# Seven products instead of eight in a third pair of each gate and up unit, with the sums on the weights made by GpSimd

## The chip, the cores and the metric

The kernel runs on one core of a Trainium2 chip. The metric is the device time of one execution in microseconds (us). Five engines work on a core: PE (TensorE, the matrix multiplier), ACT (ScalarE), DVE (VectorE), POOL (GpSimd), and SP (SyncE), which here only issues transfers.

## The reference

One decoder layer on 256 tokens of width 2048 with 16 learned tokens ahead of them: a SwiGLU block, a mixer (differential attention beside a gated short convolution), a second SwiGLU block, a last norm. The change is in the first half of the second SwiGLU block, where gate and up are made:

```python
D_MODEL = 2048; SEQ = 256; D_FF = 5632
def swiglu_ffn(h, w_gu, w_down):
    gate, up = jnp.split(h @ w_gu, 2, axis=-1)
    return (jax.nn.silu(gate) * up) @ w_down
...
h = rms_norm(s, norm_ffn2[layer])
s = s + 0.5 * swiglu_ffn(h, ffn2_w_gu[layer], ffn2_w_down[layer])
```

All inputs are float32.

## The kernel before

Every float32 operand of a matmul is split into a high part that TensorE takes at full speed (type fp32r) and the low remainder; a product is three matmuls: high times high, low times high, high times low. Activations are split when they are made. Weights are split as they arrive: a tile `st` comes from memory by a transfer that SP issues, ACT writes the high part `wh` (a cast, line 369) and DVE the remainder `wl` (a subtraction, line 370). This is the helper `parts`. There are three buffers each for `wh` and `wl` (`W_BUFS`) and four for `st` (`ST_BUFS`).

The second block's inner width of 5632 is cut into 11 groups of 512. Group 0 is made by `linear_tok`, which on the way also writes the normalised activations `hn` (`renorm`, `Mixed.pair`). Groups 1 to 10 are made by `gate_up_mix`; one call is called a unit here. A unit makes gate and up, 512 columns each, for 256 tokens (two halves of 128), over 2048 rows of weights. `linear_mix` takes these rows as eight pairs of 128-row chunks. For one pair the work is a product of a 2 x 2 matrix of blocks (token half by chunk, 128 x 128 each) with a 2 x 2 matrix of weight blocks (chunk by gate or up, 128 x 512 each). The string `KINDS` says for each of the eight pairs how this is done:

- D (direct): eight block products, in two tiles of four (tile c holds chunk c's rows for gate and for up). A tile is 12 matmuls.
- S: Strassen's way in Winograd's form, seven block products. The four sums on the activations are made once, in `Mixed.pair`, and kept as `sp`. The four sums on the weights are made anew in every unit, in a tile `tt` that takes one of the four `st` buffers (lines 507 to 510; the third needs the first, the fourth needs the third). Its products come in four tiles: one of 3 matmuls and three of 6. The last two tiles are cast from `tt`.

The results of all pairs add up in eight PSUM banks, named 1 to 7 and x. `left` counts the products that a bank is still to get; at the last one `done` evicts it (lines 522 to 543, on ACT and DVE), most of them in pair 7. The sigmoid and two products for the whole unit (`gated`, lines 546 to 548) follow in the next unit's first pair, and the result is transposed on PE (`back`, lines 561 to 566) in that next unit's last pair.

`step` and `AHEAD` put the casts of two further tiles ahead of a tile's matmuls in program order; a framework then makes a fixed order for each engine and the semaphores. After groups 0 to 3, 4 to 7 and 8 to 10 stands the product with `w_down` for that third (`linear_tok`, named pd). Behind the last units GpSimd's queue holds two loads of the last norm's gains (`gfin`, line 928).

Of the kernel before, what the change touches and what calls it, by code (L numbers as in the profile page):

```python
# [36 lines left out]
WARM = 6  # L37
HOLD = 3
LATER_AT = (4, 6)
KINDS = "DDDSDDDS"  # L40
AHEAD = 2


# [1 line left out]
def decoder_layer(ctx: ExitStack, tc: tile.TileContext, t, out):  # L45
    nc = tc.nc
# [7 lines left out]
    def bank(name):  # L54
        return psum.tile([P, 512], F32, tag="acc", name=name)
# [179 lines left out]
    def step(use):  # L235

        ahead.append(use)
        drain(AHEAD)
# [62 lines left out]
    def flush():  # L301
        while pending:
            pending.pop(0)()
# [61 lines left out]
    def parts(src, n=2):  # L365

        wh = wpool.tile([P, 2, GW], F32R, tag="wh", name="wh")[:, :n, :]
        wl = wpool.tile([P, 2, GW], F32R, tag="wl", name="wl")[:, :n, :]
        nc.scalar.copy(out=wh, in_=src)  # L369
        nc.vector.tensor_sub(wl, src, wh.bitcast(F32))  # L370
        return wh, wl
# [49 lines left out]
    class Mixed:  # L421
# [6 lines left out]
        def pair(self, p, f):  # L428
# [4 lines left out]
            nc.vector.tensor_sub(tl[:, :, 1, :], f, tl[:, :, 0, :].bitcast(F32))  # L433
            if KINDS[p] == "S":
                a11, a12, a21, a22 = (f[:, c, i * P : (i + 1) * P] for i in range(2) for c in range(2))
# [13 lines left out]
    def linear_mix(a, w, cols, name, done):  # L449

        nd, ns = KINDS.count("D"), KINDS.count("S")
        left = {k: 2 * nd * (k in "234x") + ns * (k != "x") for k in "1234567x"}
        ps = {}

        def product(k, left_op, wh, wl):
            first = k not in ps
            if first:
                ps[k] = bank(name + k)
            left[k] -= 1
            hi, lo = left_op
            nc.tensor.matmul(ps[k], hi, wh, start=first, stop=False)  # L467
            nc.tensor.matmul(ps[k], lo, wh, start=False, stop=False)  # L468
            nc.tensor.matmul(ps[k], hi, wl, start=False, stop=left[k] == 0)  # L469
            if left[k] == 0:  # L470
                done(k, ps[k])

        def use(p, n, products):

            for k, left_op, wh, wl in products:
                product(k, left_op, wh, wl)
            if p == len(KINDS) - 1 and n in (1, 2) and later:
                later.pop(0)()
            if n == (1 if KINDS[p] == "D" else 3):
                if p == 0:  # L480
                    flush()
                if side:
                    side.pop(0)()

        for p, kind in enumerate(KINDS):
            st = wpool.tile([P, 2, 2, GW], F32, tag="st", bufs=ST_BUFS, name="st")
            rows = w[2 * p * P : (2 * p + 2) * P, :].rearrange("(c p) f -> p c f", p=P)
            for q in range(2):
                nc.sync.dma_start(out=st[:, :, q, :], in_=rows[:, :, cols[q] : cols[q] + GW])
            (a11, a21), (a12, a22) = ([a.block(2 * p + c, i) for i in range(2)] for c in range(2))  # L490
            if kind == "D":
                tiles = [
                    (st[:, c], (("2", a1, 0), ("3", a1, 1), ("4", a2, 0), ("x", a2, 1)))
                    for c, (a1, a2) in enumerate(((a11, a21), (a12, a22)))
                ]
            else:
                s1, s2, s3, s4 = a.sums[p]
                tt = wpool.tile([P, 4, GW], F32, tag="st", bufs=ST_BUFS, name="tt")
                tiles = [
                    (st[:, 1, 1:2, :], (("3", s4, 0),)),  # L500
                    (st[:, :, 0, :], (("1", a11, 0), ("2", a12, 1))),
                    (tt[:, 2:4, :], (("6", s2, 0), ("4", a22, 1))),
                    (tt[:, 0:2, :], (("5", s1, 0), ("7", s3, 1))),
                ]
            for n, (src, products) in enumerate(tiles):
                if kind == "S" and n == 2:
                    nc.vector.tensor_add(tt[:, 0, :], st[:, 0, 0, :], st[:, 0, 1, :])
                    nc.vector.tensor_add(tt[:, 2, :], tt[:, 0, :], st[:, 1, 1, :])
                    nc.vector.tensor_add(tt[:, 3, :], tt[:, 2, :], st[:, 1, 0, :])
                    nc.vector.tensor_add(tt[:, 1, :], st[:, 0, 1, :], st[:, 1, 1, :])  # L510
                wh, wl = parts(src, src.shape[1])
                products = [(k, left_op, wh[:, j, :], wl[:, j, :]) for k, left_op, j in products]
                step(lambda p=p, n=n, products=products: use(p, n, products))

    def gate_up_mix(a, w_gu, g, m, gi):
# [3 lines left out]
        def done(k, ps):  # L519
# [21 lines left out]
            elif k == "7":  # L541
# [10 lines left out]
                pending.append(gated)  # L552

        linear_mix(a, w_gu, (g * GW, F + g * GW), "pg", done)

    def back(act, g, mt, k):
# [421 lines left out]
```

## Time and profile before

| | |
|---|---|
| time, median of 3 runs (lowest to highest) | 2226.62 us (2225.67 to 2226.89) |
| profiled execution, its own time | 2225.46 us |
| span of the profiled execution (first to last instruction) | 2223.7 us |
| mean granted TensorE clock | 0.998 |
| busy: PE, DVE, ACT, POOL | 2205.9, 1376.3, 998.2, 6.4 us |
| the ten units with the down products between them | 1535 to 2150 us of the span |

Busy shares are of the whole span; the stages differ. "Idle before" is time that an engine stood still ahead of an instruction, and behind the arrow stands what ended it. In the windows, each engine's busy time is followed by its number of instructions. A matmul's duration is longer than the time until the next one can start, since they are pipelined; the spacing of starts is what counts. L370 is line 370 of the kernel.

### The profile page before, as it was taken

The page shows a single profiled execution, that of the slowest core. Times are in us where ns is not written, and L with a number is a line of the kernel's source. Part 1 is how long each engine was busy: PE and PEld are TensorE (multiplying, and loading weights), DVE is VectorE, ACT ScalarE, POOL GpSimd, SP SyncE. Part 2 cuts the span into 40 slices and gives each one's busy share as a digit, 9 for nine tenths or more (in the row PEclk, how much of TensorE's full clock was granted, in tenths as well). Part 3 has the DMA queues.
Part 4 walks back from the last instruction along what each step waited for, and adds up shares of the span by engine and source line. Part 5 has one row for each costly group of instructions (what it writes and reads, how often), then busy time and mean ns, then how long its engine had stood idle before and what let it go on. Part 6 is the DMA issues. An engine that isn't in the chain of part 4 may idle for free.

```text
span 2223.7 us, 33100 instructions
## 1 busy us (share of the span) xinstructions
PE 2205.9 (99%) x13608; PEld 1989.5 (89%) x13608; DVE 1376.3 (62%) x1792; ACT 998.2 (45%) x1244; POOL 6.4 (0%) x17
## 2 busy tenths in 40 slices
PE   9999999999999999999999999999999999999998
PEld 8999999999999999898988888888888888888886
DVE  7555554455555565667765554668776578846875
ACT  6444343334434443444444444455454445534544
POOL 0000000000000000000000000000000000000000
PEclk9999999999999999999999999999999999999999
DMA  7555455555555455444555555555566555665563
GB/s 233 176 180 176 171 172 178 181 171 171 176 180 175 171 171 186 156 142 144 170 189 189 190 189 189 177 184 172 188 200 200 187 190 189 208 211 182 178 225 113
DMA packets 192023, 401.95 MB, mean 181 GB/s; under 512 B 8676, under 2 KB 8736, under 8 KB 191872
## 3 DMA queue, kind: packets, MB, share of 16 engines
q1 hardware_dynamic: 191232, 398.49, 53.0%
q8 instruction: 106, 1.74, 0.3%
q0 software_dynamic: 544, 1.21, 0.2%
q14 instruction: 45, 0.37, 0.0%
q10 hardware_dynamic: 96, 0.14, 0.0%
HBM read 397.71 MB, written 2.10 MB: 180 GB/s over the span
## 4 chain that ended last, share of the span: by engine, by line
PE 97%; DVE 1%; ACT 1%; DMA 0%; issue 0%; ACTq 0%; DVEq 0%
PE pg L467 5%; PE pg L469 5%; PE pg L468 5%; PE pg L282 4%; PE pg L280 4%; PE pd L282 4%; PE pu L282 4%; PE pu L280 4%; PE pg L281 4%; PE pd L280 4%; PE pd L281 4%; PE pu L281 4%; PE pd L320 4%; PE pd L318 4%; PE pd L319 4%; PE o L278 3%
## 5 line engine op out<-in xcount | busy, mean ns | idle before, releaser
L271 DVE TENSOR_TENSOR wl<-st,wh 128x1024 fp32r<-128x1024 f32 x392 | 478.5, 1223 | 442.4 <-ACT wh L270 442.1
L270 ACT CAST wh<-st 128x1024 fp32r<-128x1024 f32 x392 | 411.4, 1050 | 613.9 <-PE pd L281 146.9
L370 DVE TENSOR_TENSOR wl<-st,wh 128x1024 fp32r<-128x1024 f32 (+1 forms) x360 | 426.9, 1192 | 280.0 <-ACT wh L369 279.1
L369 ACT CAST wh<-st 128x1024 fp32r<-128x1024 f32 (+1 forms) x360 | 368.3, 1030 | 472.3 <-PE pgx L468 154.9
L280 PE MATMUL pg<-h,wh 128*128 128x272 f32 x704 | 203.3, 290 | 2.0 <-ACT wh L270 2.0
L280 PE MATMUL pu<-h,wh 128*128 128x272 f32 x704 | 203.3, 289 | 0.0
L282 PE MATMUL pu<-h,wl 128*128 128x272 f32 x704 | 203.0, 288 | 0.0
L282 PE MATMUL pd<-m,wl 128*128 128x272 f32 x704 | 203.0, 288 | 0.0
L280 PE MATMUL pd<-m,wh 128*128 128x272 f32 x704 | 202.9, 288 | 0.0
L281 PE MATMUL pd<-m,wh 128*128 128x272 f32 x704 | 202.4, 288 | 0.0
L281 PE MATMUL pu<-h,wh 128*128 128x272 f32 x704 | 202.4, 288 | 0.0
L281 PE MATMUL pg<-h,wh 128*128 128x272 f32 x704 | 202.4, 288 | 0.0
L282 PE MATMUL pg<-h,wl 128*128 128x272 f32 x704 | 201.1, 290 | 0.0
L467 PE MATMUL pg<-wh,hn 128*128 128x512 f32 x420 | 163.6, 390 | 0.0
L468 PE MATMUL pg<-wh,hn 128*128 128x512 f32 x420 | 163.5, 389 | 0.0
L469 PE MATMUL pg<-wl,hn 128*128 128x512 f32 x420 | 160.3, 391 | 0.0
L318 PE MATMUL pd<-wh,m 128*128 128x512 f32 x352 | 137.6, 391 | 0.0
L319 PE MATMUL pd<-wh,m 128*128 128x512 f32 x352 | 137.0, 389 | 0.0
L320 PE MATMUL pd<-wl,m 128*128 128x512 f32 x352 | 135.9, 390 | 0.0
L280 PEld LDWEIGHTS pg<-h,wh 128*128 128x128 f32 x704 | 132.9, 189 | 2.3 <-ACT wh L270 2.3
L281 PEld LDWEIGHTS pg<-h,wh 128*128 128x128 f32 x704 | 133.3, 189 | 0.0
L281 PEld LDWEIGHTS pu<-h,wh 128*128 128x128 f32 x704 | 132.7, 189 | 0.0
(279 smaller groups left out, 4536.4 us busy)
## 6 DMA issues: line engine op xcount, KB each, us to landing
st<-in_ffn_w_gu_dram SPq DMA_DIRECT2D x184, 512.0 KB, 4.3
st<-in_ffn_w_down_dram SPq DMA_DIRECT2D x88, 1024.0 KB, 5.1
st<-in_ffn_w_gu_dram SPq DMA_DIRECT2D x84, 1024.0 KB, 4.8
st<-in_w_in_dram SPq DMA_DIRECT2D x48, 1024.0 KB, 5.1
st<-in_w_gate_dram SPq DMA_DIRECT2D x64, 512.0 KB, 4.3
st<-in_w_branch_dram SPq DMA_DIRECT2D x32, 512.0 KB, 4.5
st<-in_w_out_dram SPq DMA_DIRECT2D x16, 1024.0 KB, 5.0
xin<-in_x_dram SPq DMA_DIRECT2D x8, 256.0 KB, 7.3
```

The costliest lines, as they stand in the source:

```text
L270: nc.scalar.copy(out=wh[:, :m, :], in_=sw)
L271: nc.vector.tensor_sub(wl[:, :m, :], sw, wh[:, :m, :].bitcast(F32))
L280: nc.tensor.matmul(a, wh[:, i, f], act.part(c, 0, t0, t1), start=first, stop=False)
L281: nc.tensor.matmul(a, wh[:, i, f], act.part(c, 1, t0, t1), start=False, stop=False)
L282: nc.tensor.matmul(a, wl[:, i, f], act.part(c, 0, t0, t1), start=False, stop=last)
L318: nc.tensor.matmul(ps, hi, wh[:, q, :], start=first, stop=False)
L319: nc.tensor.matmul(ps, lo, wh[:, q, :], start=False, stop=False)
L369: nc.scalar.copy(out=wh, in_=src)
L370: nc.vector.tensor_sub(wl, src, wh.bitcast(F32))
L467: nc.tensor.matmul(ps[k], hi, wh, start=first, stop=False)
L468: nc.tensor.matmul(ps[k], lo, wh, start=False, stop=False)
L469: nc.tensor.matmul(ps[k], hi, wl, start=False, stop=left[k] == 0)
```

## The change

Pairs 2, 5 and 7 of each unit are S instead of pairs 3 and 7, so there are five D pairs and three S pairs. `Mixed.pair` follows `KINDS` and makes the activation sums for pairs 2, 5 and 7. The four sums on the weights are issued to GpSimd instead of VectorE, with the same operands and in the same place in the program.

```diff
-KINDS = "DDDSDDDS"
+KINDS = "DDSDDSDS"
...
                 if kind == "S" and n == 2:
-                    nc.vector.tensor_add(tt[:, 0, :], st[:, 0, 0, :], st[:, 0, 1, :])
-                    nc.vector.tensor_add(tt[:, 2, :], tt[:, 0, :], st[:, 1, 1, :])
-                    nc.vector.tensor_add(tt[:, 3, :], tt[:, 2, :], st[:, 1, 0, :])
-                    nc.vector.tensor_add(tt[:, 1, :], st[:, 0, 1, :], st[:, 1, 1, :])
+                    nc.gpsimd.tensor_add(tt[:, 0, :], st[:, 0, 0, :], st[:, 0, 1, :])
+                    nc.gpsimd.tensor_add(tt[:, 2, :], tt[:, 0, :], st[:, 1, 1, :])
+                    nc.gpsimd.tensor_add(tt[:, 3, :], tt[:, 2, :], st[:, 1, 0, :])
+                    nc.gpsimd.tensor_add(tt[:, 1, :], st[:, 0, 1, :], st[:, 1, 1, :])
```

## The prediction, made before the result was known

> **What bounds the kernel now.** I read the profile page first (busy times, chain), then the stage that the change touches (windows by unit, waits, DVE in order of time), then rows for single prices.
>
> ```profile
> span 2223.7 us, 33100 instructions
> PE 2205.9 (99%) x13608; PEld 1989.5 (89%) x13608; DVE 1376.3 (62%) x1792; ACT 998.2 (45%) x1244; POOL 6.4 (0%) x17
> ...
> PE 97%; DVE 1%; ACT 1%; DMA 0%; issue 0%; ACTq 0%; DVEq 0%
> ```
>
> The chain that ended last runs on PE for 97% of the span, and GpSimd (POOL) does almost nothing. So a matmul less is worth its spacing, unless DVE or ACT becomes late. DVE's 62% is a mean over stages; in the stage of the change it is otherwise. These windows are one gate and up unit each, from one unit's first transposes to the next one's:
>
> ```profile
> core 0: us, PE busy (x) PEld busy (x) DVE busy (x) ACT busy (x) POOL busy (x), PEclk, DMA share, GB/s
> 1574.96:1618.91 43.95, 43.53 (x197) 35.47 (x195) 35.38 (x41) 22.23 (x26) 0.00 (x0) 1.00 0.56 191
> 1618.91:1662.94 44.03, 43.61 (x197) 35.47 (x195) 35.43 (x41) 22.28 (x26) 0.00 (x0) 1.00 0.57 190
> ...
> 1603.11 0.39 PE L467 MATMUL pg<-wh,hn 128*128 128x512 f32 x1
> 1615.80 0.39 PE L469 MATMUL pg<-wl,hn 128*128 128x512 f32 x1
> ...
> 1662.94 0.44 PE mt_ps L561 x4
> ```
>
> A unit takes 44.0 us, DVE is busy for 35.4 of them (80%) and ACT for 22.3. Between the two matmul rows lie 56 spacings without a gap, so one is 12.69 / 56 = 0.2266 us (its 0.39 is latency). A unit now has six D pairs of 24 matmuls and two S pairs of 21, which is 186, and two groups of four transposes of 0.44: 42.15 + 0.88 = 43.03 us. About 0.95 us a unit is stall. The waits of this stage say where:
>
> ```profile
> ACT wh L369 <- DVE tt L509: 21.3, 7, 3.2
> PEld pg L467 <- ACT wh L369: 6.2, 14, 0.8
> PE pg L467 <- ACT wh L369: 2.1, 5, 0.4
> ```
>
> Seven times (there are seven units that follow directly on another) ACT waits for the last add, L509, and PE then waits for ACT. DVE in order of time, across the end of one unit and into the next, shows why:
>
> ```profile
> 1619.24 1.23 DVE L370 TENSOR_TENSOR wl<-tt,wh 128x1024 fp32r<-128x1024 f32 x1 [0.20 <-ACT wh L369]
> 1620.38 0.68 DVE L532 TENSOR_TENSOR cgate<-pg,cup 128x512 f32<-128x512 f32 x1
> 1620.98 0.68 DVE L566 TENSOR_TENSOR m<-mt_ps,m 128x512 fp32r<-128x512 f32 x1
> 1621.58 1.21 DVE L370 TENSOR_TENSOR wl<-st,wh 128x1024 fp32r<-128x1024 f32 x1
> 1622.71 0.68 DVE L534 TENSOR_TENSOR u2x<-pg,cup 128x512 f32<-128x512 f32 x1
> 1623.31 0.68 DVE L566 TENSOR_TENSOR m<-mt_ps,m 128x512 fp32r<-128x512 f32 x1
> 1623.91 0.68 DVE L536 TENSOR_TENSOR cgate<-pg,u2x 128x512 f32<-128x512 f32 x1
> 1624.51 1.21 DVE L370 TENSOR_TENSOR wl<-st,wh 128x1024 fp32r<-128x1024 f32 x1
> ...
> 1633.18 1.22 DVE L548 TENSOR_TENSOR cup<-cup,cgate 128x1024 f32<-128x1024 f32 x1
> 1634.31 1.82 DVE L370 TENSOR_TENSOR wl<-st,wh 128x1024 fp32r<-128x1024 f32 x2
> 1636.05 0.68 DVE L507 TENSOR_TENSOR tt<-st 128x512 f32<-128x512 f32 x1
> ...
> 1639.62 0.68 DVE L509 TENSOR_TENSOR tt<-tt,st 128x512 f32<-128x512 f32 x1
> ```
>
> From 1619.2 on DVE starts its next work as it ends the last (0.60 us apart for 512 columns, 1.13 for 1024): the evictions of the finished unit between the subtractions (wl) of the next. It gets to the adds at 1636 and ends them at 1640.3.
>
> **Part 1: one product of eight goes.** Pair 2 and pair 5 become S and pair 3 becomes D: five D and three S, 183 matmuls. Three matmuls fewer in each of ten units: 30 x 0.2266 = 6.8 us off PE. That is all that can come directly.
>
> **Part 2: DVE and ACT per unit.** Eight adds leave DVE (8 x 0.60 = 4.8 us). One D pair (two subtractions, 2.27 us) becomes an S pair (one of 512 and three of 1024, 4.0 us). DVE gets 3.1 us lighter. ACT has 1.6 us more of casts in a unit where it is idle for half: nothing. The wait for L509 on DVE goes, at most 0.95 x 7 = 6.6 us; I take 6.3. But the first S pair now stands at pair 2, 5.4 us deeper in the burst of evictions. From 1620.4 DVE has twelve eviction instructions (10 x 0.60 + 2 x 1.13 = 8.3), eight subtractions of D0, D1 and S2 (8.5): 16.8 us. PE in that time has four transposes, S7's last tile, D0, D1 and S2 (0.44 + 1.36 + 10.88 + 4.76 = 17.4 us). That fits barely: 0 to 1 us late, I take 0.5 in seven units, +3.5.
>
> **Part 3: the price of an add on GpSimd.** No arithmetic on two tensors runs there now. The nearest rows:
>
> ```profile
> masks.py:199 POOL TENSOR_SCALAR_AFFINE_SELECT ident<-ident 128x128 f32<-128x128 f32 x1 | 0.3, 313 | 0.1
> masks.py:197 POOL MEMSET ident<- 128x128 f32 x1 | 0.2, 205 | 0.3 <-POOLq L967 0.3
> L967 POOL MEMSET const-float32-1.0<- 128x1 f32 x1 | 0.1, 99 | 0.0
> ```
>
> From the memsets, an element written costs (205 - 99) / 127 = 0.83 ns; with one read as well, (313 - 99) / 127 = 1.69. For 512 elements that is 0.52 us (write only, too low), 0.96 (one read), and with a second read at another 0.85 ns, 1.40. I take 1.18 us, between the last two: 12 adds a unit are 14.2 us of GpSimd. The Trainium skill, GPSIMD Engine Reference, section Performance versus the Vector engine, gives 4497 ns for such an add of 2048 elements, by which 512 would be an estimated 1.12 us; no run here shows it yet.
>
> By itself this chain of four (4.7 us) is hidden. A pair's weights land 4.3 us after issue (below); the adds need only these and a free tt buffer, and GpSimd's queue holds nothing ahead.
>
> ```profile
> 1616.30 0.89 SPq L489 DMA_DIRECT2D st<-in_ffn_w_gu_dram  x2
> 1620.49 0.88 SPq L489 DMA_DIRECT2D st<-in_ffn_w_gu_dram  x2
> st<-in_ffn_w_gu_dram SPq DMA_DIRECT2D x184, 512.0 KB, 4.3
> ```
>
> The four st buffers go round in order (1616.30 follows the last reading of S7's st, 1620.49 that of its tt at 1620.47). In the new order S2's weights take S7's st, land at about 1620.7, and its adds end at 1625 to 1628, when ACT wants them only after D1's last matmul (1620.7 + 0.44 + 1.36 + 10.88 = 1633.4). S7's adds start when S5's st is released, and have 10 us. If this cover were gone, ACT would stop with every cast behind it, as it does now for L509. On GpSimd's queue also stand the two gfin loads (L928). They go out in a down stage, where no adds are queued behind them; even behind the last add they would land long before their first reader at 2179.7. The extra sums of activations (four of 0.28 us, a cast, a subtraction of 0.68) fall in the stage of unit 0, where PE has 0.15 us of stall in 39.5 but DVE is at 91%: nothing, at most 1.8 us once.
>
> ```profile
> 1989.65 0.54 POOL L928 DMA_DIRECT2D gfin<-in_norm_final_dram  x1 [4.87 <-PE pd L320]
> L942 DVE TENSOR_TENSOR sT<-sT,gfin x8: 681/686/693, 2179.7 to 2214.4; 128x512 f32<-128x512 f32 x8
> 1495.00:1534.50 39.50, 39.35 (x180) 32.40 (x179) 35.77 (x66) 24.83 (x34) 0.00 (x0) 1.00 0.55 187
> ```
>
> **Part 4: do GpSimd's adds hold up DVE?** Both read SBUF. No row shows arithmetic on both at once, so the price lies between nothing and the whole 14.2 us a unit added to DVE. I take the middle case, in which an add and a DVE instruction with two SBUF inputs take turns, whole instructions at a time, while DVE instructions that read one input from PSUM run beside an add. The reason is how little decides: with nothing else late, the unit is about 1 us shorter, so it needs 1 us of stall out of 14.2 us of adds to be lost, beside a DVE that is continuously busy for 17 us of each unit. The Trainium skill, SBUF — State Buffer, section Who interferes with whom, states such a rule against this change: a DVE instruction with two SBUF inputs contends with a GpSimd instruction that reads SBUF, and the later one waits for the whole of the other. No run here shows it so far.
>
> Worked out for the two places where DVE has no slack. First the burst: adds from 1620.7 meet L532 and L566 (PSUM, no turn), delay the subtraction at 1621.58 by 0.3, run beside L534 to L536, delay the one at 1624.51 by 0.6, and end beside L538 and L542: about 1.0 us, in seven units, +7. Second, S5: the buffer for S7's sums is S5's st, free when S5's second tile is subtracted, so the four adds fall on S5's last two tiles and D6's first. There a tile lasts six matmuls, 1.36 us, and needs a cast and a subtraction within three buffers:
>
> ```profile
> L370 DVE TENSOR_TENSOR wl<-st,wh 128x1024 fp32r<-128x1024 f32 x340 | 413.6, 1221 | 272.4 <-ACT wh L369 271.6
> L369 ACT CAST wh<-tt 128x1024 fp32r<-128x1024 f32 x40 | 41.0, 1050 | 43.2 <-PE pgx L468 22.0 <-DVE tt L509 21.3
> ```
>
> Counted from the first matmul of S5: third tile cast 0 to 1.05, subtracted 1.1 to 2.3, needed 2.5; fourth needed 3.85, D6's first 5.2. If subtraction and add alternate, subtraction first, the fourth comes 0.8 late and D6's first 1.0 later still: 1.8 us. If an add gets in first, 0.75 + 1.0 + 1.0 = 2.75. I take 2.0 in ten units, +20. S5's own adds fall on D3 and D4, where a tile has 2.72 us and 3 us of slack: nothing.
>
> Sum: -6.8 - 6.3 + 3.5 + 7 + 20 = +17.4 us. The profiled execution took 2225.46 us (span 2223.7 and 1.8 around it), 1.2 below the median of 2226.62, so I add it to both and give 2243 us.
>
> **The rivals.** (A) No collision: DVE's rows keep 1.22 us beside the adds. Then -6.8 - 6.3 + 3.5 = -9.6, 2217 us; with pair 2 on time 2213. For it: ACT and DVE stream beside each other now at unchanged durations (1050 and 1221 over hundreds). Against: that is another engine. 0.25.
> (B) Collision, but mostly where DVE has slack (subtractions always first, a stall of 1 us a unit): the product is paid back, 2222 to 2231. 0.10.
> (C) DVE becomes the bound: nothing overlaps, and DVE's 31.7 us (8.3 + five D at 2.27 + three S at 4.0) plus 14.2 plus some 2 of unavoidable waits for casts make 47.9 a unit, 3.9 more than now: 2265. 0.10. Decides if adds take 1.4 us or PSUM evictions wait too.
> (D) Adds come late: a chain over 10 us makes ACT wait before tt in each S pair; 2 us in each of 30 pairs less the 9.6 won would be 2276. Needs adds of 2.5 us, beyond the rows: 0.02.
> The change does what it says; the product is surely gone.
>
> **Numbers.** Forecast case 0.53, with 2231 to 2258 (S5 at 1.0 to 2.75, the burst at 0.5 to 2). A difference of 0.2% (4.5 us) is what a measurement here tells from none. Faster: A, 0.25. Same: B, 0.10. Slower: forecast, C and D, 0.65. The range takes A's sum less its late pair on one side and C on the other: 2213 to 2265.
>
> **What would show it.** L467 to L469 at 610 each instead of 620; POOL with 120 adds of about 1.2 us. Right if the DVE subtractions of S5's last tiles and after a unit's end show 1.5 to 2.4 us or idle time before them, and unit windows are about 46 us. Wrong if these rows stay at 1.22 and units are 43 us (A), or if ACT's wait for POOL tt is the longest wait (D).

## The result, and the profile after

The changed kernel takes 2254.2 us (median of 4, 2252.86 to 2254.83) against 2226.57 us: a ratio of 1.0124, 95% interval [1.0106, 1.0141], 27.6 us slower. The forecast was 2243 (2213 to 2265), slower. The profiled execution took 2254.47 us with a span of 2252.7, 29.0 longer than before.

The page of the changed kernel: span, busy times, the chain that ended last.

```profile
span 2252.7 us, 33235 instructions
PE 2210.9 (98%) x13578; PEld 1982.0 (88%) x13578; DVE 1409.2 (63%) x1737; ACT 1015.8 (45%) x1265; POOL 224.1 (10%) x137
...
PE 91%; DVE 5%; ACT 2%; issue 1%; DMA 0%; ACTq 0%; DVEq 0%
```

PE has 30 matmuls fewer (13608 before), three in each of ten units, as it should. But the chain leaves PE: 8% of the span is now DVE, ACT and issue (2% before). DVE has 55 instructions fewer and is busy 33 us longer. POOL's 120 adds take 220 us, 1.84 each on average, where 120 x 1.18 = 142 were forecast.

The waits of the stage (us in total, times, longest):

```profile
PEld pg L469 <- DVE wl L370: 46.0, 51, 1.9
PE pg L469 <- DVE wl L370: 25.9, 37, 1.5
```

Two whole units, from second group of transposes to second group, as windows (length, then PE, weight loads, DVE, ACT and POOL in us, granted clock, DMA share, GB/s):

```profile
1582.95:1629.52 46.57, 43.95 (x192) 34.71 (x191) 36.91 (x35) 24.03 (x28) 20.96 (x12) 1.00 0.53 181
1629.52:1675.30 45.78, 43.74 (x193) 34.71 (x192) 37.26 (x35) 24.05 (x28) 21.99 (x12) 1.00 0.53 182
```

ACT's wait for the last add is gone. In its place PE waits for `wl`, the remainder that DVE subtracts: its weight loads 51 times, its matmuls 37 times. A unit takes 46.2 us on average of these two, 44.0 before. The groups of the changed kernel (us busy, mean ns of one):

```profile
L508 POOL TENSOR_TENSOR tt<-tt,st 128x512 f32<-128x512 f32 x30 | 60.9, 2030 | 0.0
L370 DVE TENSOR_TENSOR wl<-tt,wh 128x1024 fp32r<-128x1024 f32 x60 | 90.1, 1528 | 37.4 <-ACT wh L369 37.4
```

The range of a subtraction and of an add in the same kernel, by source line (ns, min/median/max):

```profile
L370 DVE TENSOR_TENSOR wl<-tt,wh x60: 1210/1226/2359, 1551.6 to 2171.9; 128x1024 fp32r<-128x1024 f32 x60
L508 POOL TENSOR_TENSOR tt<-tt,st x30: 1287/2268/2284, 1534.7 to 2160.8; 128x512 f32<-128x512 f32 x30
```

An add takes 1.29 us when nothing meets it and 2.27 when something does; a subtraction 1.22 (as before) or 2.36. Each grows by about the other's length. Pair 5 of a unit (called the fifth pair here), in order of time: POOL, DVE and PE.

```profile
1614.89 2.27 POOL L508 TENSOR_TENSOR tt<-tt,st 128x512 f32<-128x512 f32 x1
1617.24 2.15 POOL L509 TENSOR_TENSOR tt<-tt,st 128x512 f32<-128x512 f32 x1
...
1613.80 4.45 DVE L370 TENSOR_TENSOR wl<-tt,wh 128x1024 fp32r<-128x1024 f32 x2 [1.54 <-ACT wh L369]
1618.17 4.04 DVE L370 TENSOR_TENSOR wl<-st,wh 128x1024 fp32r<-128x1024 f32 x3
...
1616.07 0.50 PE L469 MATMUL pg<-wl,sp 128*128 128x512 f32 x1 [0.72 <-DVE wl L370]
1618.30 0.50 PE L469 MATMUL pg<-wl,sp 128*128 128x512 f32 x1 [0.57 <-DVE wl L370]
1620.53 0.50 PE L469 MATMUL pg<-wl,hn 128*128 128x512 f32 x1 [0.57 <-DVE wl L370]
```

Two subtractions take 4.45 us, and PE is stopped three times, 2.23 us apart: one subtraction and one add in turn (a subtraction's spacing is 1.13, which leaves 1.10 for the add). A matmul's record of 0.39 us covers 0.16 of each stop (spacing 0.2266), so the three stops are 0.72 + 0.57 + 0.57 + 3 x 0.16 = 2.3 us.

### The profile page after: what moved, and what is told of

Its sections match the earlier page's. It is cut to its first block, busy times and chain, and to the rows that moved or that the text cites. A ratio compares the mean times of both kernels' runs of the same rounds, so it can differ in the third digit from the quotient of the medians.

```text
span 2252.7 us, 33235 instructions
## 1 busy us (share of the span) xinstructions
PE 2210.9 (98%) x13578; PEld 1982.0 (88%) x13578; DVE 1409.2 (63%) x1737; ACT 1015.8 (45%) x1265; POOL 224.1 (10%) x137
## 3 DMA queue, kind: packets, MB, share of 16 engines
q0 software_dynamic: 544, 1.21, 0.2%
## 4 chain that ended last, share of the span: by engine, by line
PE 91%; DVE 5%; ACT 2%; issue 1%; DMA 0%; ACTq 0%; DVEq 0%
PE pg L469 4%; PE pg L282 4%; PE pg L280 4%; PE pu L282 4%; PE pd L282 4%; PE pg L281 4%; PE pu L280 4%; PE pd L280 4%; PE pu L281 4%; PE pd L281 4%; PE pg L468 4%; PE pg L467 4%; PE pd L320 3%; PE pd L318 3%; PE pd L319 3%; DVE wl L370 3%
## 5 line engine op out<-in xcount | busy, mean ns | idle before, releaser
L370 DVE TENSOR_TENSOR wl<-st,wh 128x1024 fp32r<-128x1024 f32 (+1 forms) x360 | 460.1, 1287 | 275.0 <-ACT wh L369 274.1
L507 POOL TENSOR_TENSOR tt<-st 128x512 f32<-128x512 f32 x30 | 47.6, 1588 | 1938.9 <-DMA st<-in_ffn_w_gu_dram 1721.6
L469 PE MATMUL pg<-wl,hn 128*128 128x512 f32 x390 | 150.5, 398 | 15.1 <-DVE wl L370 15.0
L467 PE MATMUL pg<-wh,hn 128*128 128x512 f32 x390 | 152.2, 390 | 0.0
L468 PE MATMUL pg<-wh,hn 128*128 128x512 f32 x390 | 152.1, 390 | 0.0
```

## The experiments

Ten runs, all beside the kernel before. The theory: a GpSimd add and a VectorE instruction, each with two inputs from SBUF, take turns, and that costs where VectorE has no slack. The first rival: the third S pair is itself too tight.

**One half of the change: sums on VectorE.**

```diff
-KINDS = "DDDSDDDS"
+KINDS = "DDSDDSDS"
```

> One half of the change alone: three S pairs, the sums stay on VectorE. Theory (turn-taking: each GpSimd add holds up a VectorE instruction that reads two SBUF operands): no add runs beside a subtraction any more, every subtraction is back at 1.22 us and no wait for one by PE is longer than 0.3 us in the fifth pair; VectorE has 12 adds of 0.60 a unit more. Product -6.8, adds late after a unit's end (2.4 us more work in a burst that was full) about +1.8 in seven units, a little in the fifth pair: 2224 to 2236 us. Rival (the third S pair itself, two S pairs with one D between them and the first one pair earlier, is what PE waits for): stays at 2245 to 2256, or goes higher since VectorE has more work.

2250.42 us (ratio 1.0108, [1.0093, 1.0124]): 14 us above the theory's range, and inside the rival's (2245 to 2256). By its time alone this run would speak for the rival; the run without sums, below, decides against it. No subtraction is long any more (1.23 us at most), so the collisions are gone; another wait has come:

```profile
ACT wh L369 <- DVE tt L509: 55.3, 14, 5.9
```

PE in the order of time, at the burst:

```profile
1595.52 0.79 PE L467 MATMUL pg<-wh,sp 128*128 128x512 f32 x1 [2.95 <-ACT wh L369]
```

Windows there, and at the next unit's burst (the granted clock is the third figure from the end of a row):

```profile
1595.50:1598.00 2.50, 2.48 (x6) 2.00 (x7) 2.50 (x3) 2.23 (x3) 0.00 (x0) 0.50 0.84 291
1598.00:1600.00 2.00, 2.00 (x7) 1.52 (x6) 1.59 (x2) 0.68 (x1) 0.00 (x0) 0.50 0.40 153
...
1644.30:1650.00 5.70, 5.68 (x25) 4.58 (x26) 5.70 (x5) 3.84 (x5) 0.00 (x0) 1.00 0.55 185
```

The four adds stand behind the burst of evictions; ACT, waiting for the last one, holds every cast behind it for up to 5.9 us, and PE stops for 2.95. In this unit the clock was then granted at 0.50 until about 1601.6, so matmuls came every 0.43 us: the unit took 48.8 us. The next unit had the same stop at the full clock (last row) and took 46.0. So the third product costs about as much with its sums on VectorE as on GpSimd, by another wait and a slower clock.

**The other half: two S pairs, sums on GpSimd.**

> The other half alone: pairs 3 and 7 are S as before, the sums are made by GpSimd. Theory (turn-taking): the adds get their buffer when the first D pair, or the fourth pair, is cast, so they fall on D pairs, where a tile has some 3 us of slack; the wait for the last add (0.9 us in seven units) goes, up to 1 us a unit comes back in the burst after a unit's end: 2218 to 2228 us, although GpSimd adds of 1.3 to 2.3 us run beside VectorE all the same. Rival (sums on GpSimd are slow wherever they stand: late, or they slow everything down): above 2235 us, two thirds of the 27.6 us, since two thirds of the adds are left.

2238.04 us (1.0054, [1.0039, 1.0069]): 10 us above the theory's range, and above 2235, where the rival put it. Where the adds fell shows why. POOL, DVE and PE after a unit's end:

```profile
1630.12 2.27 POOL L508 TENSOR_TENSOR tt<-tt,st 128x512 f32<-128x512 f32 x1
...
1628.92 2.31 DVE L370 TENSOR_TENSOR wl<-st,wh 128x1024 fp32r<-128x1024 f32 x1
...
1631.29 0.73 PE L469 MATMUL pg<-wl,hn 128*128 128x512 f32 x2 [0.83 <-DVE wl L370]
1636.99 0.50 PE L469 MATMUL pg<-wl,hn 128*128 128x512 f32 x1 [0.65 <-DVE wl L370]
```

The sums for pair 3 run beside D1 and D2, while VectorE is still in the burst; a D pair there has no slack. Nothing stops PE at the adds for pair 7, so sums on GpSimd are not slow wherever they stand, as the rival had it. I had taken "D pair" for "slack".

**No sums at all.** The last two tiles of an S pair are cast from `st`.

> Three S pairs and no sums on the weights at all: the last two tiles of an S pair are cast from the weights themselves, so the gate and up values are not those of the reference. Theory (turn-taking): without adds nothing holds up a subtraction: -6.8 for the product, -6.3 for today's wait, +3.5 for the first S pair in the burst: 2213 to 2219 us. Rival (third S pair itself): 2240 us or more.

2214.95 us (0.995, [0.9934, 0.9967]), within the theory's 2213 to 2219. The third S pair by itself is sound: a unit takes 42.48 us and PE does not stop in it, which rules the first rival out.

```profile
1575.91:1618.39 42.48, 42.48 (x192) 35.03 (x191) 32.25 (x35) 24.07 (x28) 0.00 (x0) 1.00 0.59 198
```

**Writes without reads.**

```diff
-                    nc.gpsimd.tensor_add(tt[:, 0, :], st[:, 0, 0, :], st[:, 0, 1, :])
+                    for _ in range(2):
+                        nc.gpsimd.memset(tt[:, 0, :], 1.0)
```

(and so for the other three)

> As the changed kernel, but each GpSimd add is replaced by two GpSimd memsets of the same 128x512 (so the sums are not those of the reference): GpSimd is busy about as long (1.0 us for 1.3) at about the same places and writes SBUF, but reads nothing. Theory (an add and a VectorE instruction take turns over what both read): subtractions stay at 1.22 us, 2213 to 2221 us, like the kernel without sums. Rival (anything that GpSimd does to SBUF, or its semaphores, holds VectorE up): subtractions of 1.5 to 2.4 us again and 2235 us or more.

2216.06 us (0.9955, [0.9941, 0.997]), as expected. The group of the writes:

```profile
L508 POOL MEMSET tt<- 128x512 f32 x58 | 30.7, 529 | 479.1 <-DVE wl L370 479.1
```

The range of a subtraction in this run:

```profile
L370 DVE TENSOR_TENSOR wl<-tt,wh x60: 1212/1224/1226, 1548.6 to 2133.9; 128x1024 fp32r<-128x1024 f32 x60
```

GpSimd works beside the same subtractions (71 of those with 1024 columns overlap a memset), and none exceeds 1.23 us. So GpSimd's writes do not hold VectorE up, nor do the waits that this run keeps; a memset does not wait for the weights to land, as an add or a copy does.

**One read.** Each add becomes a copy of one block.

> As the changed kernel, but each GpSimd add is a GpSimd copy of one of the four weight blocks into tt (the sums are left out, so the values are not those of the reference). GpSimd now reads one operand of 512 and writes one. With memsets, which read nothing, VectorE's subtractions stayed at 1.22 us. Theory (they take turns over reading SBUF): subtractions that meet a copy are longer again, 1.4 us and more, and the third S pair loses part of its gain: 2220 to 2245 us, between the kernel with memsets (2216) and the change (2254). Rival (only an instruction that reads two operands is in VectorE's way): 2214 to 2218 us and all subtractions at 1.22.

2221.45 us (0.9981, [0.9972, 0.9991]), inside the theory's range near its low end, 5.4 above the memsets.

```profile
L510 POOL COPY tt<-st 128x512 f32<-128x512 f32 x29 | 37.6, 1296 | 0.0
```

The subtraction beside the copies:

```profile
L370 DVE TENSOR_TENSOR wl<-tt,wh x60: 1208/1226/1665, 1547.5 to 2137.5; 128x1024 fp32r<-128x1024 f32 x60
```

A copy is 0.61 us when alone (this group's mean is 1.30); of the subtractions that overlap one, 29 take 1.4 us or more, 1.67 at most. So one operand read from SBUF by GpSimd is enough.

**The adds for pair 7 moved from pair 5 to pair 6.**

```diff
-ST_BUFS = 4
+ST_BUFS = 3
...
-                tt = wpool.tile([P, 4, GW], F32, tag="st", bufs=ST_BUFS, name="tt")
+                tt = wpool.tile([P, 4, GW], F32, tag="tt", bufs=1, name="tt")
```

> The changed kernel, with one buffer of its own for tt and three instead of four for st. So the sums for pair 7 get their buffer when pair 5's last tile is subtracted, and the four adds move from pair 5's tiles to those of pair 6 (D), where a tile has 2.7 us instead of 1.4. Theory (turn-taking, and only where VectorE has no slack does it cost): PE's three waits in the fifth pair (0.72 + 0.57 + 0.57 and 3 x 0.16 us of latency not counted, 2.3 us in each of ten units) go; the collisions after a unit's end stay: 2228 to 2236 us. Rival (three adjacent S pairs are tight anyway): within 4 us of the changed kernel, 2250 to 2258.

2243.56 us (1.0079, [1.0064, 1.0094]): 10.6 less than the change, about half of what was expected, and outside both ranges. PE's three stops in the fifth pair are gone, a new wait is there:

```profile
1618.46 2.15 POOL L509 TENSOR_TENSOR tt<-tt,st 128x512 f32<-128x512 f32 x1
...
1620.64 1.05 ACT L369 CAST wh<-tt 128x1024 fp32r<-128x1024 f32 x1 [3.40 <-POOL tt L509]
...
1622.23 0.66 PE L561 MATMUL mt_ps<-ident,cup 128*128 128x128 f32 x4 [1.10 <-ACT u2x L522]
```

Taking turns, four adds need 8.3 us (1612.30 to 1620.61), more than one D pair's 5.4. They end late, ACT waits 3.4 us, and an eviction (u2x) stands behind it that frees PE's bank. With one buffer fewer for `st`, no cast of this stage waits for a transfer of weights.

**Besides, pair 2's sums back on VectorE; then the gate later too.** In both, pair 2's adds are issued to VectorE. In the second, the finished unit's gate is emitted after pair 3 instead of pair 0:

```diff
-                if p == 0:
-                    flush()
+                if p in (0, 3):
+                    flush(p > 0)
```

(`flush(False)` leaves the gate in its list.)

> As the run with a buffer of its own for tt, and besides the sums of pair 2 go back to VectorE; those of pairs 5 and 7 stay on GpSimd. Theory: no add is left where VectorE is full, so no subtraction at the start of a unit is longer than 1.3 us; but VectorE has four adds (2.4 us) more there, and with all sums on VectorE PE stood still for 2.95 us at that place in seven units: 2215 (no sums) + 7 x 3.2 = 2237, between 2230 and 2242. If the adds of pairs 5 and 7 cost as much where they now stand as they did before: 2255 or more.

> As the run before it, and the gate of the finished unit (a sigmoid on ScalarE, two multiplications of 1024 on VectorE, 2.26 us) is put after pair 3 instead of pair 0 of the next unit, out of the burst. Theory: the wait at pair 2 falls by about these 2.3 us, to below 1 us: 2215 to 2225 us, under the kernel before. Rival (VectorE's total, not its burst, is the limit in these units): no better than 2232.

2264.42 us (1.0177, [1.0162, 1.0193]) and 2250.86 us (1.0112, [1.0097, 1.0127]). Both miss, by 22 and 26 us above the top of their ranges, and both lie where their rivals put them (2255 or more, 2232 or more). The first joins the two late waits: 2.95 us at pair 2 (and again a clock of 0.93 over a whole unit) and 1.1 at pair 7. In the second, VectorE's order shows what the move did:

```profile
1591.60 1.22 DVE L550 TENSOR_TENSOR cgate<-cgate,u2x 128x1024 f32<-128x1024 f32 x1
1592.74 0.68 DVE L512 TENSOR_TENSOR tt<-tt,st 128x512 f32<-128x512 f32 x1
...
1594.63 0.50 PE L469 MATMUL pg<-wh,sp 128*128 128x512 f32 x1 [2.11 <-ACT wh L371]
```

The framework put one of the gate's multiplications ahead of the last add all the same; PE stops for 2.11 us instead of 2.95, here at the full clock. So this run does not decide between the burst and VectorE's total: the burst was not emptied.

**The kernel before with the gate after pair 4; then with pair 7's sums on GpSimd.**

> The kernel before, two S pairs and all sums on VectorE, with only the gate moved, to after pair 4. If the wait for the last add (0.9 us in seven units) comes from the burst of evictions, it goes: 2218 to 2222 us, and what e7 has below this is the third product's own gain. If not: 2225 to 2228.

> The kernel before with the gate moved to after pair 4, and of its two S pairs only pair 7's sums made by GpSimd (pair 3's stay on VectorE). With both pairs on GpSimd PE's waits were all in the first three pairs of a unit, none at the adds for pair 7. Theory (collisions cost where VectorE has no slack, and nothing elsewhere): 2219 to 2224 us, as with all sums on VectorE (2221.6), though ten times four adds run on GpSimd beside VectorE. Rival (each add beside VectorE costs PE something wherever it stands; 30 pairs cost 39 us over the kernel without sums, so 1.3 us a pair): 2232 or more.

2221.59 us (0.998, [0.997, 0.999]) and 2221.89 us (0.9982, [0.9972, 0.9991]), both as expected by the theory. Waits of the first:

```profile
ACT wh L371 <- DVE tt L509: 1.7, 1, 1.7
```

The waits of PE's weight loads in the second:

```profile
PEld pg L471 <- DVE wl L372: 3.2, 15, 0.3
```

The group of an add in the second:

```profile
L511 POOL TENSOR_TENSOR tt<-tt,st 128x512 f32<-128x512 f32 x10 | 20.8, 2076 | 0.0
```

The wait for the last add falls from 21.3 to 1.7 us in total, and both versions are 0.2% faster than the kernel before. The second also shows that collisions (adds of 2.08 us instead of 1.29) are free where VectorE has time. This is the best answer to the rival of a price per add: 40 adds beside VectorE cost nothing that shows.

## Why the prediction was right, point by point

Slower was forecast with 0.65, and the case of turn-taking with 0.53 and 2231 to 2258 us; that case came, at 2254.2. The ten units together, from each one's first matmul to the next one's (or to the down product's), take 434.5 us before; with the sums (the changed kernel) and without them (the run without sums) they take:

```profile
sum 462.23, PE 436.21 PEld 345.21 DVE 363.40 ACT 240.19 POOL 202.44; mean PE 43.62 PEld 34.52 DVE 36.34 ACT 24.02 POOL 20.24
sum 423.44, PE 423.44 PEld 348.76 DVE 303.49 ACT 238.26 POOL 0.00; mean PE 42.34 PEld 34.88 DVE 30.35 ACT 23.83 POOL 0.00
```

So the adds cost 38.8 us. Comparing the two kernels matmul by matmul puts these at three places: 24.9 in and just behind the fifth pairs of all ten units, 10.8 in pairs 0 to 2 of the seven units that follow directly on another's matmuls (the first unit not among them), and 3.0 in pairs 0 to 2 of the first unit. Elsewhere the two kernels keep step.

**The product, -6.8 us:** shown. 30 matmuls went. The kernel without sums has units of 42.48 us, and the kernel before with its gate moved some 43.2 (second transposes at 1577.27 and 1620.46); the difference is 0.7, forecast 0.68.

**Today's wait, -6.3:** the mechanism is shown (moving the gate alone gives 4.5 us), the size was too high: of the seven units five took 44.0 us and two only 43.5, and without the wait they take 43.2, not 43.0. **Pair 2 in the burst, +3.5:** mis-sized; without sums PE did not stop there. Rival A's sum of -9.6 without collision stands at -11.2 (2214.95 against 2226.11).

**An add at 1.18 us:** measured 1.29 alone. "Adds of about 1.2 us" in the changed kernel did not come: taking turns, they took 1.84 on average.

**Turns, whole instructions at a time:** shown. Subtraction and add alternate; memsets do nothing, one read is enough. The exception for instructions that read one input from PSUM is seen in the trace of the changed kernel:

```profile
1631.67 2.27 POOL L510 TENSOR_TENSOR tt<-st 128x512 f32<-128x512 f32 x1
...
1630.52 2.27 DVE L370 TENSOR_TENSOR wl<-st,wh 128x1024 fp32r<-128x1024 f32 x1
1632.71 0.68 DVE L534 TENSOR_TENSOR u2x<-pg,cup 128x512 f32<-128x512 f32 x1
...
1632.85 0.50 PE L469 MATMUL pg<-wl,hn 128*128 128x512 f32 x1 [0.88 <-DVE wl L370]
```

L534 ran inside this add at its usual 0.68 us, and so did all the others of its kind that overlap an add (42, none above 0.69). This is the rule of the Trainium skill, SBUF — State Buffer, section Who interferes with whom, that the prediction set against the change; trace and runs agree with it, in that two inputs from SBUF on VectorE wait for a GpSimd instruction that reads SBUF, and not for one that only writes.

**The fifth pair, +20 (2.0 a unit, bounds 1.8 and 2.75):** right in kind, 2.5 a unit in size. Against the run without sums it is 1.8 us in two units, 2.2 and 2.4 in two and 2.7 to 2.9 in six, so both orders that the prediction worked out occur, and the dearer one most often. **Its place:** moving the adds' buffer took these stops away. **S5's own adds, "nothing":** right; between pair 2 and the fifth pair the two kernels keep step.

**The burst, +7 (1.0 in seven units):** mis-sized, 1.5 a unit. Of the two subtractions forecast as late, the first was so by 1.06 us (the 2.27 above, instead of 1.21) and not by 0.3: an add had begun 0.11 us ahead of it, and PE stopped for it. The second was late by 0.55, where 0.6 was forecast.

**The activation sums in unit 0, "nothing, at most 1.8 us once":** right for the sums themselves: the last 30.03 us ahead of the first unit's first matmul hold the same work of PE and are as long in both kernels, and without adds the first unit takes 42.47 us and PE does not stop in it. But the first unit's own first adds, which had no term in the sum, ran there beside the last normalisations, where DVE was at 91%:

```profile
1535.72 1.51 DVE L902 SCALAR_TENSOR_TENSOR hnf<-s,vec,rstd 128x256 f32<-128x256 f32 x1
1537.15 1.38 DVE L439 TENSOR_TENSOR sums<-hnf 128x128 f32<-128x128 f32 x1
...
1541.05 0.50 PE L469 MATMUL pg<-wl,hn 128*128 128x512 f32 x1 [1.17 <-DVE wl L370]
1545.34 0.50 PE L469 MATMUL pg<-wl,hn 128*128 128x512 f32 x1 [1.11 <-DVE wl L370]
```

An instruction of 128 columns takes 1.38 us instead of 0.28: it waited for a whole add. These two stops and the slow starts behind them are the 3.0 us. Where `tt` had its own buffer the first adds began 4.7 us later (1536.18 instead of 1531.48), and the two stops are not there. I priced the moved sums as instructions of DVE, and forgot that the first pair's adds on GpSimd start in that stage.

Together, in spans of the profiled executions: -11.3 (forecast -9.6) for the product, the wait and pair 2, +24.9 (20), +10.8 (7) and +3.0 (0) make +27.4; 1.3 us of the span's 29.0 already lay ahead of unit 0, which the change does not touch. The three prices of the adds were all too low, so no miss of one hid that of another, and the time came out in the upper part of the range. (From the median of 2226.62 the forecast sum gives 2244; the 2243 counts from the profiled execution.)

Rival A fell by its own condition (subtractions did not stay at 1.22), and B by the 24.9 us of the fifth pairs. D did not occur in the changed kernel but did, at a wait of ACT of up to 3.4 us a unit, where the adds were moved to pair 6. C's price of 47.9 a unit was not reached (46.2 on average): an add alone takes 1.29 us and not 1.4, and the evictions from PSUM did not wait.

## What to carry to other kernels

Moving two-input work from VectorE to GpSimd was no relief while VectorE itself read two SBUF tensors: the adds took turns with what they were to make room for, at twice the time, and were free only where VectorE had slack in that very place. Price an offload by what runs beside it, tile by tile and from the first one on, and ask what stands in order behind the engine that waits for it. And look at the burst of evictions before looking for a product to save: moving the gate (a sigmoid and two multiplications) out of it gained 4.5 us here, while the third product gained nothing in any of the kernels that make its sums.

## What was not expected of the hardware

With all sums on VectorE, PE stopped for 2.7 to 3.0 us in each of seven units. After six of these stops matmuls ran at a granted clock of 0.50, for 3.4 us and once for 6.8, and after one they did not. Units with it were up to 2.8 us longer (48.8 and 46.0); over the run the mean clock was 0.993 against 0.998.

The times at which the clock changes in this run lie whole multiples of 3.413 us apart (1594.74, 1820.02 and 1867.81, for example, are 66 and 14 of them apart). In windows of that grid PE's busy time, ahead of the first stop shown and around the second, is:

```profile
1591.33:1594.74 3.41, 1.24 (x5) 0.48 (x3) 2.95 (x5) 0.32 (x1) 0.00 (x0) 1.00 0.23 90
...
1639.12:1642.53 3.41, 2.25 (x10) 1.30 (x8) 3.38 (x6) 0.00 (x0) 0.00 (x0) 1.00 0.57 220
1642.53:1645.95 3.42, 1.63 (x7) 1.27 (x8) 2.23 (x3) 2.73 (x3) 0.00 (x0) 1.00 0.46 123
```

The first stop left 2.17 us of one window without a matmul, and the clock fell at that window's end, 1594.74. The second was as long but fell across two windows, 1.16 us in one and 1.79 in the next, and the clock stayed. In the run with the gate put after pair 3, two stops of nearly the same length came out differently, too, and the second of them lay whole in one window:

```profile
1592.80:1596.21 3.41, 1.58 (x7) 1.22 (x8) 3.36 (x5) 2.68 (x3) 0.00 (x0) 1.00 0.46 117
1596.21:1599.63 3.42, 3.42 (x17) 2.82 (x16) 3.42 (x4) 2.17 (x3) 0.90 (x1) 1.00 0.49 190
...
1910.24:1913.65 3.41, 1.30 (x6) 0.79 (x5) 3.36 (x4) 1.63 (x2) 0.00 (x0) 1.00 0.35 80
1913.65:1917.07 3.42, 3.42 (x9) 2.63 (x8) 3.42 (x4) 2.26 (x3) 0.00 (x0) 0.50 0.75 289
```

Over the gate and up units of the three runs with such stops, all eleven windows at full clock with 2.11 us or more of recorded idle time were followed by the lower clock, and none with 1.83 us or less. Stops of 1.5 us and less in the changed kernel left it at 1.00. The Trainium skill, TensorE: Matmul & The Clock Gate, section Part 1: The HAM clock gate (the "warmup" mystery), has the clock watched in free-running windows of about 3.4 us and halved after an idle one. The windows and half the clock agree with these traces, but a window need not be idle throughout: 2.11 of 3.41 us were enough.
